# Padding the activation tiles by 64 bytes and shifting the low weight tiles by 32 in a float32r transformer kernel

## The chip, the cores and the metric

The kernel runs on one core of one Trainium2 chip. Its metric is the time of one launch on the device in microseconds (us). Before the change two timed runs took 3197.18 and 3197.62 us, a median of 3197.4 us.

## What is computed

Two layers of a first block (a state-space mixer beside multi-head latent attention, cross attention to a memory, a gated feed-forward network), then one layer of a second block (a compressed and windowed attention beside a dilated one, merged by gates), on 256 tokens of 2048 features in float32. Nearly all the work is products of 256 tokens with large weight matrices:

```python
proj = h @ w_in[l]                                   # 2048 x 3664
x = x + jnp.concatenate([y_ssd, y_mla], -1) @ w_out[l]
x = x + memory_cross_attention(h, m, w_xq[l], ...)
x = x + swiglu(h, w_gate[l], w_up[l], w_down[l])     # 2048 x 5632, twice, and back
...
proj = h @ w_in                                      # second block, 2048 x 11056
out = (sigmoid(ma) * ya + sigmoid(mb) * yb) @ w_out
```

## The kernel before

Each float32 operand of a long product is split into a high part of type float32r and a low part, the rest, also float32r. A product is then three matmuls into the same PSUM bank: high by high, high by low and low by high.

**Weights.** A block of a weight matrix comes by a transfer of SyncE's queue into a tile `raw` (pool `rawp`, 5 buffers). ScalarE copies it to `wh` (line 411) and VectorE subtracts that from `raw` to make `wl` (line 412). `wh` and `wl` come from one pool `wp`, 4 buffers for each name. A tile has 1024 elements, 4096 bytes, on each of 128 partitions.

**Activations.** A pair of tiles `xh`, `xl` holds 512 features of all 256 tokens, features on the partitions: 4 chunks of 256 tokens, 4096 bytes (pool `xp`, 6 buffers for each name, made by `pair`).

**The products.** `block` makes the products with the tokens on the output's partitions: the moving operand is a half of the weight tile, `wh[:, j]` or `wl[:, j]` with j = 0 or 1 (512 columns, 2048 bytes; where the block is 296 or 280 columns wide, the second half starts 1184 or 1120 bytes after the first), and the stationary operand is 128 tokens of a chunk of `xh` or `xl`, 512 bytes. It runs lines 423, 424 and 425 for the two token halves m of each j, so that six matmuls on j = 0 are followed by six on j = 1 (the last block of a product takes all of m = 0 first). `block_fm` is the other way round, for the state-space mixer's convolution inputs: 128 columns of weights are stationary and the 256 tokens of a chunk move (lines 461 to 463).

**Other work.** Norms, attention and the scan are cut into steps, "tasks", which `tick` places between the matmuls of the long products. The order on TensorE is the order in which the program is written; the other engines' order is made by a scheduler from priorities, and split work has a high one. Small temporaries come from pools `t2` (9 buffers of 2048 bytes) and `t1` (6 buffers, NT1). `t1` serves, among others, the convolution (line 791: a tile `u` of 3 + 256 columns whose first three GpSimd clears at line 792; lines 793 to 801 use it) and the block summaries of the second block (line 1321: copies of slices of `kc`, which TensorE then transposes at line 377).

**Where the tiles lie.** Pools take their memory one after the other, with the same address on every partition. By the built program, in bytes, with the distance between buffers:

| tile | before | after |
|---|---|---|
| `x`, the residual | 25,376 | 25,376 |
| `after_r`, a constant of the scan (line 887) | 44,384 | 44,384 |
| `raw` | 45,536 + 4096 i | 45,536 + 4096 i |
| `wh` | 66,016 + 4096 i | 66,016 + 4096 i |
| `wl` | 82,400 + 4096 i | 82,432 + 4096 i |
| `xh` | 98,784 + 4096 i | 98,816 + 4160 i |
| `xl` | 123,360 + 4096 i | 123,776 + 4160 i |
| slots (`ff`, `kc` and others) | 147,936 + 4096 i | 148,736 + 4096 i |
| `t2` | 197,088 + 2048 i | 197,888 + 2048 i |
| `t1` | 215,520 + 1056 i, i to 5 | 216,320 + 1056 i, i to 4 |

Modulo 512 bytes, `raw`, `wh`, `wl`, `xh`, `xl`, the slots and `t2` are all at 480 before the change. `x` is at 288, which is 192 below that, and `after_r` is at 352, which is 128 below.

Of the kernel before, what the change touches and what calls it, by code (L numbers as in the profile page):

```python
# [11 lines left out]
F32 = mybir.dt.float32  # L12
F32R = mybir.dt.float32r
# [6 lines left out]
P = 128  # L20
S = 256
# [6 lines left out]
NSLOT, NT2, NT1 = 12, 9, 6  # L28
# [6 lines left out]
# ---------------------------------------------------------------- host layout  # L35
# [6 lines left out]
def _tile_a(w, width=512):  # L42
    """[L, K, N] -> [L, N/width, K/512, 2, 128, 2, width]; one [128, 2, width] block per transfer."""
    L, K, N = w.shape
    w = w.reshape(L, K // 512, 2, 2, P, N // width, width)
    return np.ascontiguousarray(w.transpose(0, 5, 1, 2, 4, 3, 6))


def _tile_b(w):
    """[L, 2048, N] -> [L, N/128, 2, 128, 8, 128]."""  # L50
    L, K, N = w.shape
    w = w.reshape(L, 2, 8, P, N // P, P)
    return np.ascontiguousarray(w.transpose(0, 4, 1, 3, 2, 5))


def _cols(v):
    """[n*128] -> [128, n]"""
    return v.reshape(-1, P).T


def _rows(v):
    """[n] -> [128, n], the same row on every partition"""
    return np.broadcast_to(v.reshape(1, -1), (P, v.size))


def _feature_major(x):
    """[256, 2048] -> [128, 16, 256]"""
    return np.ascontiguousarray(x.T.reshape(16, P, S).transpose(1, 0, 2))


def _token_major(x):
    """[256, n] -> [128, 2, n]"""
    return np.ascontiguousarray(x.reshape(2, P, -1).transpose(1, 0, 2))
# [19 lines left out]
def _head_order_a():  # L93
    """Position p of a query head of branch a: pairs (g, g + 1) of key groups with one r."""
    return [(2 * (c // 4) + i) * 4 + c % 4 for c in range(8) for i in range(2)]
# [64 lines left out]
def _layout(a):  # L160
    """Every array that goes to the chip, in the order and the shape it is read."""
# [6 lines left out]
    w = a["w_in"]  # L168
# [5 lines left out]
    L = DEPTH  # L174
# [48 lines left out]
# ---------------------------------------------------------------- the program  # L223


class _Task:
    """Work beside the long products, cut into steps; a step yields the number of ticks to wait."""
# [5 lines left out]
class _Net:  # L233
    def __init__(self, ctx, tc, I, out, poff, coff):
        self.tc = tc
        self.nc = nc = tc.nc
        self.I = I
        self.out = out
        self.poff, self.coff = poff, coff
        self.now = 0  # L240
        self.ready = []
        self.tasks = []
        pool = lambda name, bufs, **k: ctx.enter_context(tc.tile_pool(name=name, bufs=bufs, **k))
        self.one = pool("one", 1)
        self.rawp = pool("rawp", 5)
        self.wp = pool("wp", 4)
        self.xp = pool("xp", 6)
        self.sp = pool("sp", NSLOT)
        self.k2 = pool("k2", NT2)
        self.k1 = pool("k1", NT1)  # L250
        self.sm = pool("sm", 1)
        self.psw = pool("psw", 4, space=PSUM)
        self.psm = pool("psm", 4, space=PSUM)
        ctx.enter_context(tc.manual_schedule(engines={mybir.EngineType.PE}))
        self.par = self.one.tile([P, I["params"].shape[1]], F32, name="par")
        self.cst = self.one.tile([P, I["consts"].shape[1]], F32, name="cst")
        self.x = self.one.tile([P, 2, D], F32, name="x")
        self.junk = self.one.tile([P, 512], mybir.dt.bfloat16, name="junk")
        self.mhalf = self.one.tile([P, 1], F32, name="mhalf")
        nc.gpsimd.memset(self.mhalf, -0.5)  # L260
        self.ident = self.c("ident")

    # -- tasks
# [17 lines left out]
    def get(self, t):  # L281
        """the result of a task, a list of them, or the value itself"""
        if isinstance(t, _Task):
            while not t.done:
                self.tick()
            return t.result
        return t
# [6 lines left out]
    # -- small things  # L294
# [30 lines left out]
    def rsqrt(self, out, ss, width):  # L325
        """out = (ss / width + eps) ** -0.5"""
        nc = self.nc
        n = ss.shape[1:]
        t = self.small([P] + list(n), name="rs" + "_".join(map(str, n)), bufs=2)
        nc.vector.tensor_scalar(t, ss, 1.0 / width, EPS, op0=OP.mult, op1=OP.add)  # L330
        mh = self.mhalf
        for _ in range(len(n) - 1):
            mh = mh.unsqueeze(1)
        nc.gpsimd.tensor_tensor(out, t, mh.to_broadcast([P] + list(n)), op=OP.pow)  # L334

    def squares(self, src, acc):
        """acc = sum of src ** 2 along the free axis"""
        self.nc.scalar.activation(self.junk[:, :src.shape[1]], src, AF.Square, accum_out=acc)

    def head_squares(self, src, acc, heads):  # L340
        """acc [128, heads] = sum of squares of every head's columns of src [128, 512]"""
        j = self.t2([P, 512])
        self.nc.scalar.activation(j, src, AF.Square)
        self.nc.vector.tensor_reduce(acc, j.rearrange("p (h d) -> p h d", h=heads), axis=AX.X, op=OP.add)

    # -- operands of the long products

    def pair(self):
        h = self.xp.tile([P, 4, S], F32R, name="xh", tag="xh")
        l = self.xp.tile([P, 4, S], F32R, name="xl", tag="xl")  # L350
        return h, l

    def hi_lo(self, pair, c, n, src, gain=None, imm=None):
        """chunks c .. c+n of a pair from src [128, n, 256], times a gain by partition"""
# [17 lines left out]
    def two_transposed(self, srcs):  # L372
        """srcs: two functions of the token tile giving [128 tokens, 128]; a bank [128, 2, 256]"""
# [9 lines left out]
    def transposed(self, src, gain=None, imm=None):  # L383
        """src(m) -> [128 tokens, 512]; a task for its four chunks, feature-major, as a pair"""
# [8 lines left out]
    def weights(self, src, n, w):  # L393
        """one block [128, n, w] from DRAM, split into high and low parts"""
# [6 lines left out]
    def weight_tiles(self, n, w):  # L401
        raw = self.rawp.tile([P, n, w], F32, name="raw", tag="raw")
        h = self.wp.tile([P, n, w], F32R, name="wh", tag="wh")
        l = self.wp.tile([P, n, w], F32R, name="wl", tag="wl")
# [9 lines left out]
    def block(self, pairs, srcs, w=512, hold=HOLD):  # L414
        """token-major products: two banks [128 tokens, w]; the last weights serve one bank, then the other"""
# [35 lines left out]
    def block_fm(self, pairs, src):  # L451
        """feature-major products for 128 columns: one bank [128 features, 256 tokens]"""
# [15 lines left out]
    # -- the residual stream  # L468
# [24 lines left out]
    # -- start  # L493

    def start(self):
        """the first operands, in the order they are needed"""
# [44 lines left out]
    def angles(self):  # L541
        """cosines and sines of every rotary embedding"""
# [45 lines left out]
    def rope_gains(self, l, which):  # L588
        """rotary tables with the gain of the rotated part folded in"""
# [12 lines left out]
    def rotate(self, out, x, ct, st):  # L602
        """out, x [128, ..., 2 * half] (up to three free axes), tables broadcast to the same shape"""
# [12 lines left out]
    # -- attention of one head  # L616

    def soft(self, s, mask, scale_of, spans):
        """spans [(lo, hi)] by query tile over the columns of a bank; returns exp and 1/sum"""
# [29 lines left out]
    def probs_t(self, e):  # L649
        """probabilities [128, 384] transposed: keys by [tile 0: all tokens | tile 1: second half]"""  # L650
# [9 lines left out]
    def scores(self, s, parts):  # L660
        """s [128, 384]; parts [(qT [k, 256], kT [k, 256])] sum over the contraction"""
# [6 lines left out]
    # ------------------------------------------------------------ block 1  # L668
# [72 lines left out]
    def rms_bank(self, r):  # L741
        """a column by token tile, as rows on every partition"""
# [13 lines left out]
    def ssd_steps(self, l, krd):  # L756
        """softplus of the step sizes, and the decays by step"""
# [48 lines left out]
    def ssd_scan(self, l, cb, dt, a):  # L806
# [24 lines left out]
        # masked c . b, state positions on the partitions  # L831
# [9 lines left out]
        # state after the first chunk  # L841
# [19 lines left out]
        def decays(m, g):  # L861
            """rows of summed decays for 8 heads"""
# [84 lines left out]
    def mla_queries(self, l, qa_t, rqa):  # L947
        """[nope heads 0-3, nope heads 4-7, rope of all heads] before the norm; -scale/rms by (tile, head)"""
# [68 lines left out]
    def mla_heads(self, l, hp, q, nsc, kn, kr, v):  # L1017
        """two heads: chunks of the pair that four heads share"""
# [38 lines left out]
    # -- attention to the memory  # L1057
# [34 lines left out]
    def head_rms(self, t, name):  # L1092
        """t [128, 2, 512]: 1/rms by (tile, head of 128)"""
# [84 lines left out]
    # -- feed forward  # L1178
# [45 lines left out]
    # ------------------------------------------------------------ block 2  # L1224
# [29 lines left out]
    def x_fm(self, nb):  # L1254
        """512 features of x times their gain, feature-major"""
# [9 lines left out]
    def h2_pair(self, nb, xt, rb):  # L1265
        """512 features of rms(x) * g_pre * (1 + scale) + shift"""
# [19 lines left out]
    def rope_part(self, t, c0, heads, dh, rot, tabs):  # L1286
        """rotate the first rot of every head's dh columns of t[:, :, c0:...] in place"""
# [3 lines left out]
    def gate_fm(self, pairs, src):  # L1291
        """twice silu of 4 feature-major chunks"""
# [10 lines left out]
    def plain_t(self, src, out):  # L1303
        """out [128, 4, 256] = four chunks of src(m), feature-major"""
# [5 lines left out]
    def summaries(self, t, c0, which, vc):  # L1310
        """block summaries of the columns c0.. (4 groups of 64) of t: [128 (group, 32), 64]"""
# [70 lines left out]
    def branch_a_inputs(self, pairs):  # L1382
# [11 lines left out]
        # a quarter of 1 + tanh: the gate, halved against the doubled silu  # L1394
# [7 lines left out]
    def branch_a_cmp(self, tasks, qt, ga, kcr):  # L1402
        """probabilities over the block summaries, gated: [128 (group, 32), r, tokens]"""
# [54 lines left out]
    def branch_a_heads(self, c, kts, qt, ks, kt, ga, cmp, vcr, zf):  # L1458
        """the two query heads of chunk c"""
# [43 lines left out]
    def branch_b(self, pairs, nb):  # L1503
        """inputs of 4 heads"""
# [35 lines left out]
    def gate_rows(self):  # L1540
        """gate * g_post along the free axis"""
# [136 lines left out]
```

## Time and profile before

| | |
|---|---|
| timed runs | 3197.18 and 3197.62 us |
| profiled execution, span | 3196.7 us |
| TensorE matmuls (PE) busy | 3175.3 us, 99% |
| TensorE weight loads (PEld) busy | 2656.9 us, 83% |
| VectorE (DVE) busy | 2034.1 us, 64% |
| ScalarE (ACT) busy | 1553.8 us, 49% |
| GpSimd (POOL) busy | 53.4 us, 2% |
| transfers | 625.28 MB, 196 GB/s |

Busy times of an engine are shares of the span in which at least one of its instructions runs. A matmul's recorded duration reaches past the start of the next, since matmuls are pipelined; times of one line therefore add up to more than the span. In a timeline the first column is the start of a row in us from the span's start and the second its duration.

### The profile page before, as it was taken

The numbers are of one execution on the slowest core, as the hardware profiler recorded it, in microseconds if no ns is written. First come the engines' busy times: TensorE is split into PE (matmuls) and PEld (weight loads), VectorE is DVE, ScalarE is ACT, GpSimd is POOL, SyncE is SP. The second block draws the span as 40 slices with busy tenths as digits, with TensorE's granted clock in tenths as the row PEclk, the third lists the DMA queues.
The fourth block names the chain that finished last, engine by engine and source line by source line (L and its number), as shares of the span: only waits on it lengthen the run. The fifth ranks groups of instructions, "written<-read, shape, count | busy, mean of one in ns | idle before, by whom it ended". The sixth has DMA issues, their size and how long they took to land.

```text
span 3196.7 us, 41513 instructions
## 1 busy us (share of the span) xinstructions
PE 3175.3 (99%) x15705; PEld 2656.9 (83%) x15705; DVE 2034.1 (64%) x3015; ACT 1553.8 (49%) x2191; POOL 53.4 (2%) x77
## 2 busy tenths in 40 slices
PE   9999999999999999999999999999999999999998
PEld 8987888888888889887888888888878977888887
DVE  6886665555555566885767677766765555455554
ACT  7465564444444455474654444444454455444443
POOL 0010000000000000010000000000000000000000
PEclk9999999999999999999999999999999999999999
DMA  8554555555555556454567777777746533555454
GB/s 299 172 169 145 186 172 187 192 192 191 192 187 192 191 175 189 159 183 141 190 228 265 266 270 270 253 250 269 269 143 219 174 105 99 179 184 180 162 184 151
DMA packets 175160, 625.28 MB, mean 196 GB/s; under 512 B 19696, under 2 KB 19952, under 8 KB 174704
## 3 DMA queue, kind: packets, MB, share of 16 engines
q1 hardware_dynamic: 173952, 620.26, 58.2%
q8 instruction: 123, 2.02, 0.3%
q10 hardware_dynamic: 1008, 2.37, 0.2%
q14 instruction: 77, 0.63, 0.1%
HBM read 620.46 MB, written 2.10 MB: 195 GB/s over the span
## 4 chain that ended last, share of the span: by engine, by line
PE 96%; DVE 1%; DMA 1%; issue 1%; POOL 0%; ACT 0%; SPq 0%; DVEq 0%; POOLq 0%; ACTq 0%
PE pw L423 27%; PE pw L425 27%; PE pw L424 27%; PE pw L461 2%; PE pw L462 2%; PE pw L463 2%; PE mb L377 2%; PE mb L665 2%; DMA wada<-w_ada 1%; PE mb L1493 1%; PE mb L1346 0%; PE mb L903 0%; DVE wl L412 0%; PE mb L1496 0%; PE mb L887 0%
## 5 line engine op out<-in xcount | busy, mean ns | idle before, releaser
L412 DVE TENSOR_TENSOR wl<-raw,wh 128x1024 fp32r<-128x1024 f32 (+3 forms) x1069 | 1285.6, 1204 | 969.7 <-ACT wh L411 967.2
L411 ACT ACTIVATE wh<-raw 128x1024 fp32r<-128x1024 f32 (+3 forms) x1069 | 1114.9, 1043 | 1384.8 <-PE pw L425 1258.0
L423 PE MATMUL pw<-wh,xh 128*128 128x512 f32 (+2 forms) x3952 | 1555.4, 394 | 6.2 <-ACT wh L411 4.9
L425 PE MATMUL pw<-wh,xl 128*128 128x512 f32 (+2 forms) x3952 | 1526.3, 386 | 0.0
L424 PE MATMUL pw<-wl,xh 128*128 128x512 f32 (+2 forms) x3952 | 1524.6, 386 | 0.6 <-DVE wl L412 0.6
L423 PEld LDWEIGHTS pw<-wh,xh 128*128 128x128 f32 x3952 | 744.2, 188 | 153.3 <-ACT wh L411 4.9
L425 PEld LDWEIGHTS pw<-wh,xl 128*128 128x128 f32 x3952 | 743.1, 188 | 150.7 <-DVE xl L368 0.7
L424 PEld LDWEIGHTS pw<-wl,xh 128*128 128x128 f32 x3952 | 744.6, 188 | 141.6 <-DVE wl L412 2.1
L461 PE MATMUL pw<-xh,wh 128*128 128x256 f32 x640 | 183.2, 286 | 0.0
L463 PE MATMUL pw<-xh,wl 128*128 128x256 f32 x640 | 181.2, 283 | 0.0
L462 PE MATMUL pw<-xl,wh 128*128 128x256 f32 x640 | 181.1, 283 | 0.0
L485 DVE TENSOR_TENSOR x<-x,pw 128x512 f32<-128x512 f32 x224 | 144.9, 679 | 3.8 <-PE pw L425 3.8
L1240 DVE CUSTOM_DVE_ANT_0 wada<-wada,crow 128x1024 f32<-128x1024 f32 x96 | 117.3, 1221 | 33.9 <-DMA wada<-w_ada 33.8
L461 PEld LDWEIGHTS pw<-xh,wh 128*128 128x128 f32 x640 | 122.7, 192 | 1.3 <-issue 0.8
L462 PEld LDWEIGHTS pw<-xl,wh 128*128 128x128 f32 x640 | 122.8, 192 | 0.1
L463 PEld LDWEIGHTS pw<-xh,wl 128*128 128x128 f32 x640 | 122.7, 192 | 0.0
L630 ACT ACTIVATE t<-t,mn 128x256 f32<-128x256 f32 (+1 forms) x128 | 58.4, 457 | 63.1 <-DVE mn L627 62.3
L367 ACT ACTIVATE xh<-mb,par 128x256 fp32r<-128x256 f32 x112 | 50.9, 467 | 13.1 <-PE mb L377 12.2
L368 DVE SCALAR_TENSOR_TENSOR xl<-mb,par,xh 128x256 fp32r<-128x256 f32 x112 | 51.8, 478 | 3.7 <-ACT xh L367 2.6
L334 POOL TENSOR_TENSOR xr<-rs,mhalf 128x1 f32<-128x1 f32 x16 | 9.8, 619 | 2512.1 <-DVE rs L330 2306.4
L358 ACT ACTIVATE xh<-mb 128x512 fp32r<-128x512 f32 (+1 forms) x68 | 35.1, 516 | 30.5 <-PE mb L377 15.8
L627 DVE CUSTOM_DVE_ANT_0 t<-mb,cst 128x128 f32<-128x128 f32 x80 | 26.0, 354 | 25.8 <-PE mb L665 25.4
(358 smaller groups left out, 1564.4 us busy)
## 6 DMA issues: line engine op xcount, KB each, us to landing
raw<-w_gate SPq DMA_DIRECT2D x176, 512.0 KB, 3.6
raw<-w_up SPq DMA_DIRECT2D x176, 512.0 KB, 3.8
raw<-w_down SPq DMA_DIRECT2D x176, 512.0 KB, 3.6
raw<-w_out SPq DMA_DIRECT2D x96, 512.0 KB, 3.5
wada<-w_ada SPq DMA_DIRECT2D x96, 512.0 KB, 5.5
raw<-w_in_x SPq DMA_DIRECT2D x48, 512.0 KB, 3.9
raw<-w_in_z SPq DMA_DIRECT2D x32, 512.0 KB, 3.5
raw<-w_ma SPq DMA_DIRECT2D x32, 512.0 KB, 3.3
```

Source lines behind the costliest of these rows:

```text
L377: self.nc.tensor.transpose(t[:, j, m * P:(m + 1) * P], src(m), self.ident)
L411: nc.scalar.activation(h, raw, AF.Copy)
L412: nc.vector.tensor_tensor(l, raw, h.bitcast(F32), op=OP.subtract)
L423: nc.tensor.matmul(pt[m], lhsT=xh[:, k, ms], rhs=wh[:, j], start=c == 0, stop=False)
L424: nc.tensor.matmul(pt[m], lhsT=xh[:, k, ms], rhs=wl[:, j], start=False, stop=False)
L425: nc.tensor.matmul(pt[m], lhsT=xl[:, k, ms], rhs=wh[:, j], start=False, stop=c == 4 * n - 1)
L461: nc.tensor.matmul(pt, lhsT=h[:, j], rhs=xh[:, c], start=(k == 0), stop=False)
L462: nc.tensor.matmul(pt, lhsT=h[:, j], rhs=xl[:, c], start=False, stop=False)
L463: nc.tensor.matmul(pt, lhsT=l[:, j], rhs=xh[:, c], start=False, stop=(k == 15))
L485: self.nc.vector.tensor_tensor(xs, xs, pt[m], op=OP.add)
L665: nc.tensor.matmul(s[:, a:b], lhsT=q[:, m * P:(m + 1) * P], rhs=k[:, 0:b - a], start=(i == 0), stop=(i == len(parts) - 1))
L1240: nc.vector.tensor_tensor_reduce(out=t, in0=t, in1=self.crow[hf], scale=1.0, scalar=0.0, op0=OP.mult, op1=OP.add, accum_out=self.adap[:, j ...
```

## The change

The `wl` tiles get a pool of their own behind a gap of 32 bytes. Each `xh` and `xl` tile gets 16 more elements, 64 bytes, at its end, which nothing reads or writes. With that, the stationary operands lie at 16 different offsets, multiples of 32 bytes modulo 512, from the moving ones, where they were at one before. To make room, the pool `t1` gets 5 buffers for 6. The rest of the diff takes comments out, and lines move by up to 3.

```diff
-NSLOT, NT2, NT1 = 12, 9, 6
+NSLOT, NT2, NT1 = 12, 9, 5
...
         self.wp = pool("wp", 4)
+        self.gap = pool("gap", 1)
+        self.gap.tile([P, 8], F32, name="gap")
+        self.wl_pool = pool("wl", 4)
         self.xp = pool("xp", 6)
...
     def pair(self):
-        h = self.xp.tile([P, 4, S], F32R, name="xh", tag="xh")
-        l = self.xp.tile([P, 4, S], F32R, name="xl", tag="xl")
-        return h, l
+        return tuple(self.xp.tile([P, 4 * S + 16], F32R, name=n, tag=n)[:, :4 * S].rearrange("p (c t) -> p c t", c=4)
+                     for n in ("xh", "xl"))
...
         h = self.wp.tile([P, n, w], F32R, name="wh", tag="wh")
-        l = self.wp.tile([P, n, w], F32R, name="wl", tag="wl")
+        l = self.wl_pool.tile([P, n, w], F32R, name="wl", tag="wl")
```

The order on TensorE, ScalarE, GpSimd and SyncE's queue is the same as before. On VectorE it differs only in the block summaries of the second block. Before, in the first of the two summaries (a number behind a tile's name is that of its buffer's use):

```order
L1321 COPY t_20406<-kc 128x128
L1321 COPY t_20408<-kc 128x128
L412 TENSOR_TENSOR wl<-raw,wh 128x560 x4
L412 TENSOR_TENSOR wl<-raw,wh 128x1024 x4
L1395 TENSOR_SCALAR ga<-ga 128x96
L412 TENSOR_TENSOR wl<-raw,wh 128x1024
L1336 TENSOR_TENSOR blk<-mb,par 64x8x15 x8
L1321 COPY t_20410<-kc 128x128
L412 TENSOR_TENSOR wl<-raw,wh 128x1024
L1321 COPY t_20412<-kc 128x128
```

Now, at the same place (numbers of tiles are 7 higher, lines 2):

```order
L1323 COPY t_20413<-kc 128x128
L414 TENSOR_TENSOR wl<-raw,wh 128x560 x4
L414 TENSOR_TENSOR wl<-raw,wh 128x1024 x4
L1397 TENSOR_SCALAR ga<-ga 128x96
L414 TENSOR_TENSOR wl<-raw,wh 128x1024
L1338 TENSOR_TENSOR blk<-mb,par 64x8x15 x8
L1323 COPY t_20415<-kc 128x128
L414 TENSOR_TENSOR wl<-raw,wh 128x1024
L1323 COPY t_20417<-kc 128x128
L1323 COPY t_20419<-kc 128x128
```

One copy, of the second half of the third group, has moved from before nine splits of weight blocks to behind them, so that two copies stand together behind the next split where one did. In the second summary, some 50 us later, two copies move behind one split each.

## Rows read from the trace of the kernel before

**Rows 1.** The page, parts 1 and 2: busy us, and granted clock in 40 slices.

```profile
PE 3175.3 (99%) x15705; PEld 2656.9 (83%) x15705; DVE 2034.1 (64%) x3015; ACT 1553.8 (49%) x2191; POOL 53.4 (2%) x77
PEclk9999999999999999999999999999999999999999
```

**Rows 2.** Waits of PE: who waited for whom, us in total, times, longest.

```profile
PE pw L423 <- ACT wh L411: 4.9, 1, 4.9
...
PE pw L423 <- DVE x L485: 0.3, 1, 0.3
```

**Rows 3.** Groups of PE by shape: line, tiles, shape, count, busy us, mean ns.

```profile
L423 PE MATMUL pw<-wh,xh 128*128 128x512 f32 x3760 | 1497.9, 398 | 6.2 <-ACT wh L411 4.9 <-ACT xh L1275 1.1 <-DVE x L485 0.3
...
L461 PE MATMUL pw<-xh,wh 128*128 128x256 f32 x640 | 183.2, 286 | 0.0
...
L423 PE MATMUL pw<-wh,xh 128*128 128x296 f32 x128 | 38.7, 302 | 0.0
...
L423 PE MATMUL pw<-wh,xh 128*128 128x280 f32 x64 | 18.8, 295 | 0.0
```

**Rows 4.** Timeline of PE in the feed-forward network: start us, duration, line.

```profile
1026.74 0.39 PE L423 MATMUL pw<-wh,xh 128*128 128x512 f32 x1
...
1027.19 0.39 PE L425 MATMUL pw<-wh,xl 128*128 128x512 f32 x1
...
1030.82 0.39 PE L423 MATMUL pw<-wh,xh 128*128 128x512 f32 x1
```

**Rows 5.** Timeline of PE in the convolution's products.

```profile
99.73 0.28 PE L463 MATMUL pw<-xh,wl 128*128 128x256 f32 x1
...
101.89 0.28 PE L463 MATMUL pw<-xh,wl 128*128 128x256 f32 x1
```

**Rows 6.** Timeline of PEld, the weight loads, at the place of rows 4.

```profile
1027.19 0.19 PEld L423 LDWEIGHTS pw<-wh,xh 128*128 128x128 f32 x1
```

**Rows 7.** Timeline of PE in blocks of 296 columns, first of each six.

```profile
33.31 0.30 PE L423 MATMUL pw<-wh,xh 128*128 128x296 f32 x1
...
34.13 0.30 PE L423 MATMUL pw<-wh,xh 128*128 128x296 f32 x1
...
34.95 0.30 PE L423 MATMUL pw<-wh,xh 128*128 128x296 f32 x1
```

**Rows 8.** Timeline of PE in blocks of 280 columns, first of each six.

```profile
2394.90 0.29 PE L423 MATMUL pw<-wh,xh 128*128 128x280 f32 x1
...
2395.67 0.29 PE L423 MATMUL pw<-wh,xh 128*128 128x280 f32 x1
...
2396.44 0.29 PE L423 MATMUL pw<-wh,xh 128*128 128x280 f32 x1
```

**Rows 9.** Timeline of PE where transpositions of x and ff follow a product.

```profile
341.29 0.39 PE L425 MATMUL pw<-wh,xl 128*128 128x512 f32 x1
341.52 0.60 PE L377 MATMUL mb<-cst,x 128*128 128x128 f32 x4
...
501.25 0.39 PE L425 MATMUL pw<-wh,xl 128*128 128x512 f32 x1
501.48 0.60 PE L377 MATMUL mb<-cst,ff 128*128 128x128 f32 x4
```

**Rows 10.** Timeline of PE at the scan's decays.

```profile
152.52 1.10 PE L887 MATMUL mb<-ar,after 128*128 128x512 f32 x4
153.45 0.39 PE L423 MATMUL pw<-wh,xh 128*128 128x512 f32 x1
```

**Rows 11.** Timelines of DVE and PE at two users of t1.

```profile
1248.91 0.48 DVE L798 SCALAR_TENSOR_TENSOR t<-t,cw,t 128x256 f32<-128x256 f32 x1
1250.28 0.42 DVE L793 TENSOR_TENSOR t<-pw,t 128x256 f32<-128x256 f32 x1
...
2429.69 0.22 DVE L1321 COPY t<-kc 128x128 f32<-128x128 f32 x1
...
2431.32 0.60 PE L377 MATMUL mb<-cst,t 128*128 128x128 f32 x4
```

## The prediction

> **What bounds the kernel now.** The busy times come first: TensorE is busy for 3175.3 of 3196.7 us, and its granted clock stays in the top tenth of full speed in all 40 slices [rows 1], which is the 2.4 GHz level. Then the waits of TensorE: eleven kinds, the longest one 4.9 us in total and the shortest 0.3 us, 12.4 us together [rows 2]. So nothing that TensorE waits for is worth more than 0.4%, and the time is the number of matmuls times the distance from the start of one to the start of the next. I call that distance the step. The durations in the grouped rows are longer (398 ns for 512 columns [rows 3]) because neighbouring matmuls overlap; the step has to be read from a timeline.
>
> The grouped rows give the counts: each shape has three lines of equal count (423 to 425, or 461 to 463), so there are 3 x 3760 = 11,280 matmuls of 512 columns, 3 x 640 = 1,920 of 256, 3 x 128 = 384 of 296 and 3 x 64 = 192 of 280 [rows 3]. That is 13,776 in all. Steps: at 512 columns, the first and last row of 19 stand 4.08 us apart, 18 steps of 226.7 ns [rows 4]. At 256 columns, 19 rows stand 2.16 us apart, 18 steps of 120.0 ns [rows 5]. The sum: 11,280 x 226.7 = 2557 us, 1,920 x 120.0 = 230 us, 384 x 136.7 = 52 us and 192 x 128.3 = 25 us (the last two steps are read below), 2864 us or 90% of the span. The rest is the small attention matmuls, the transpositions and the start.
>
> The two long steps also show what is in a step. They differ by 106.7 ns for 256 columns, 0.417 ns a column, one column per cycle at 2.4 GHz. What is left at no columns is 120.0 - 106.7 = 13.3 ns. This fixed part, 13,776 x 13.3 = 183 us or 5.7% of the time, is the only thing that where the operands lie could touch. While a matmul streams its moving operand (wh or wl), the weights of the next (xh or xl) are loaded: the load recorded at 1027.19 starts as the matmul before its own does [rows 4, 6], so both read the same memory at once, and a bank collision would show up as such a fixed part.
>
> **Part one: the operands get 16 offsets.** Before, wh, wl, xh and xl all start at the same place modulo 512 bytes, and chunks, token halves and the half j of a 512-wide block are multiples of 512 apart: offset 0 in every pair. If the 13.3 ns came from that, a pair at another offset would step faster. The trace of before already holds such pairs.
>
> First, blocks of 296 columns. Half j = 1 starts 296 x 4 = 1184 bytes after j = 0, which is 160 modulo 512. Six matmuls of j = 1 run from 33.31 to 34.13 us, six of j = 0 from 34.13 to 34.95: 0.82 us each, 136.7 ns a step [rows 7]. Without the fixed part a step would be 296 x 0.417 = 123.4 ns, six of them 0.74 us. The j = 1 half does not lose it.
>
> Second, blocks of 280 columns, where j = 1 lies at 1120 bytes, 96 modulo 512. Six of j = 0 take 2394.90 to 2395.67, six of j = 1 take 2395.67 to 2396.44: 0.77 us each, 128.3 ns [rows 8], against 6 x 116.8 = 0.70 us without the fixed part.
>
> Third, a 512-column matmul during which the weights of a transposition are loaded. With weights from x, at offset 192, the step is 341.29 to 341.52; with weights from ff, at offset 0, it is 501.25 to 501.48: 0.23 us both times [rows 9].
>
> Fourth, the 512-column matmuls of line 887, with both operands in other pools and 128 between them: four take 152.52 to 153.45, 232.5 ns each [rows 10]. That is a little more than 226.7, like the 0.23 us beside a transposition at offset 0, and no trace of 213.
>
> So 0, 96, 128, 160 and 192 behave alike, both multiples of 64 and odd multiples of 32. There is a reason to expect it of the others: while 512 bytes of weights are loaded, recorded with 0.19 us [rows 6], the moving operand runs through most of its 2048 bytes in a step of 0.227 us. The distance between the two addresses grows by more than 512 bytes during one load, so whatever offset they start from, they pass through all 16. I take a gain of nothing for the change of offsets. Bounds from the same rows: a row is printed to 0.01 us, and a run of six is known to 1.7 ns a step; 13,776 x 1.7 = 23 us either way.
>
> The trace shows 226.7 ns at 512 columns. The Trainium skill, in "TensorE: Matmul & The Clock Gate", section "Back-to-back issue gap", gives a warm step of N / 2.4 + 2.5 ns, which is 215.8 at 512 and 109.2 at 256. The trace disagrees by 10.9 and 10.8 ns; by that rule nearly all of the fixed part ought to be removable, and the sum, if this change removed it, would be an estimate of 3197 - (11,280 x 10.9 + 1,920 x 10.8 + 384 x 10.9 + 192 x 9.1) / 1000 = 3048 us. Nothing in the trace ties that difference to the offset.
>
> **Part two: what else the shift touches.** The padded rows hold the same 1024 elements, and no instruction is added. The subtraction that writes wl now writes 32 bytes off from what it reads; no row shows a price for that. Its cover: VectorE is busy for 2034.1 of 3196.7 us [rows 1], so its work may take half as long again before it fills the span. I take nothing. The tiles behind xp move by 800 bytes, and the raw tiles, which take the weight transfers, not at all.
>
> **Part three: five t1 buffers instead of six.** Where does a sixth buffer matter? I set each t1 tile's first write against the last read of the tile whose buffer it now gets. Two places come out late. In the convolution the clearing of three columns on GpSimd (line 792) must now wait for the third multiply-add of the channel before, line 798, which starts at 1248.91 and takes 0.48 us. What needs the cleared tile is line 793, at 1250.28 [rows 11]: done with 0.8 us to spare, and GpSimd has nothing else queued there. In the block summaries, one more copy of 0.22 us is held on VectorE until the first transpositions have read their tiles, so that two copies stand together where the last one stood alone. It ran from 2429.69 to 2429.91; the last of two now ends about 2430.13, and the transpositions that need it start at 2431.32 [rows 11]. Queued behind it are splits of weight blocks that TensorE wants later. Cost nothing; if the cover were gone, the copy's 0.2 us, and with all of its kind below 3 us.
>
> The sum: 0 + 0 + 0 on a profiled span of 3196.7 us, whose two timed runs have a median of 3197.4. So 3197.4 us.
>
> **The rivals.** *Faster: the fixed part is a collision after all.* It would have to be one that the offsets 96, 128, 160 and 192 share with 0 and the other 11 of the 16 do not. Against it stand rows 7 to 10; for it only that the fixed part has no other visible cause and that the trace shows no pair of split operands at, say, 64 or 256. If 11 of 16 lost it: 183 x 11 / 16 = 126 us, 3071 us. If all did: 3014 us. This turns into over 2% from 64 us / 13,776 = 4.6 ns a step. (The Trainium skill's step, in the section named above, would put this case at the estimate of 3048 us.)
>
> *Slower: equal offsets are the good case.* Two streams in lock step might avoid each other, and an unequal offset cost a few ns. The nearest row for that is line 887, 232.5 against 226.7 at offset 128 [rows 4, 10]: 5.8 ns x 13,776 = 80 us, 3277 us. Against it: the steps of rows 9 are as long at offset 0, and rows 7 and 8 show no rise at 160 and 96. It decides from 4.6 ns a step, too.
>
> *A wait in place of the buffer.* If the five buffers hold up ScalarE's or VectorE's queue, TensorE sees it only after the blocks that are split ahead are used up. Against it: part three. Time: at most 3200 us, no change.
>
> **How the numbers follow.** No change, 0.9: four independent places say so, and TensorE waits for nothing that the change could lengthen. The collision rival 0.06, the lock-step rival 0.04. About 2% is what a measurement of this kernel can tell from no change, and the cases fall on its sides as named. The range is the forecast's own, 3197.4 less and plus the 23 us of the steps' resolution: 3174 to 3220; it leaves the two rivals outside, 0.10, and some of the 0.9.
>
> **What would show it.** In the profile after, the steps of 512 and 256 columns in an undisturbed stretch: 226.7 and 120.0 if I am right, 213 to 222 if the collision rival is, 230 and more for the other. If the offsets matter singly, steps would differ within one block between lines 423, 424 and 425, or from one x tile to the next. TensorE's waits should stay near 12 us, with no new one on the summaries' transpositions. I am wrong if the fixed part depends on an offset that no row here holds.

## The result, and the profile after

The changed kernel takes 3235.9 us (two runs, 3235.59 and 3236.21), against 3197.4 before: a ratio of 1.012, with a 95% interval of 1.0077 to 1.0164. It is slower by 38.5 us, which is less than 2% but more than the measurement's uncertainty, and 16 us above the end of the predicted range. The profiled execution has a span of 3233.3 us, 36.6 more than the 3196.7 of before.

The page of the kernel after, span and busy times (they answer to [rows 1]):

```profile
span 3233.3 us, 41527 instructions
...
PE 3212.4 (99%) x15705; PEld 2652.1 (82%) x15705; DVE 2036.2 (63%) x3015; ACT 1553.7 (48%) x2191; POOL 53.1 (2%) x77
```

TensorE has the same 15,705 matmuls and is busy 37.1 us longer; VectorE, ScalarE and GpSimd are within 2.1 us of before. The mean granted clock is 0.998 of full speed, the 2.4 GHz level. The waits of TensorE after, the longest and the shortest of ten kinds (as [rows 2]; a row gives us in total, times, longest):

```profile
PE pw L425 <- ACT wh L413: 5.2, 2, 4.5
...
PE mb L379 <- DVE mg L1610: 0.3, 1, 0.3
```

The ten add up to 12.1 us, where there were 12.4, and none is on the block summaries' transpositions. So TensorE does not wait longer; its steps are longer. The groups of PE by shape (as [rows 3], whose lines 423 and 461 are 425 and 463 here):

```profile
L425 PE MATMUL pw<-wh,xh 128*128 128x512 f32 x3760 | 1516.8, 403 | 6.2 <-ACT wh L413 5.2 <-ACT xh L1277 1.1
L426 PE MATMUL pw<-wl,xh 128*128 128x512 f32 x3760 | 1476.7, 393 | 0.8 <-DVE wl L414 0.8
L427 PE MATMUL pw<-wh,xl 128*128 128x512 f32 x3760 | 1476.6, 393 | 0.0
L463 PE MATMUL pw<-xh,wh 128*128 128x256 f32 x640 | 181.8, 284 | 0.0
```

The line that was 1497.9 us, 398 ns, is now 1516.8 us, 403 ns; the line of 256 columns went the other way, 183.2 to 181.8. The timeline of PE in the feed-forward network after (start us, duration, line; as [rows 4]), four rows that follow one another and the one 81 steps behind the first:

```profile
1026.10 0.40 PE L425 MATMUL pw<-wh,xh 128*128 128x512 f32 x1
1026.34 0.39 PE L426 MATMUL pw<-wl,xh 128*128 128x512 f32 x1
1026.57 0.39 PE L427 MATMUL pw<-wh,xl 128*128 128x512 f32 x1
1026.79 0.40 PE L425 MATMUL pw<-wh,xh 128*128 128x512 f32 x1
...
1044.82 0.40 PE L425 MATMUL pw<-wh,xh 128*128 128x512 f32 x1
```

81 steps take 18.72 us, 231.1 ns each, where there were 226.7. Within a triple the steps are about 0.24, 0.23 and 0.22 us: they differ by line. The convolution's products after (as [rows 5]), 42 steps apart:

```profile
99.01 0.28 PE L463 MATMUL pw<-xh,wh 128*128 128x256 f32 x1
...
103.95 0.28 PE L463 MATMUL pw<-xh,wh 128*128 128x256 f32 x1
```

That is 4.94 / 42 = 117.6 ns, where there were 120.0. At 256 columns the change is a gain.

To see where the 36.6 us are, I took every distance from one matmul's start to the next in both traces, instruction by instruction in the same order, and summed the differences by line. A step belongs to the matmul that streams while the weights of the next are loaded, so the pair of operands that meet in it is the streamed tile of one row and the loaded tile of the next:

| step of | streams, loads meanwhile | count | mean change | sum |
|---|---|---|---|---|
| L425, 512 columns | `wh`, `xh` | 3760 | +5.5 ns | +20.6 us |
| L426, 512 columns | `wl`, `xl` | 3760 | +2.7 ns | +10.2 us |
| L427, 512 columns | `wh`, `xh` of the next chunk or half | 3760 | +2.6 ns | +9.6 us |
| L463 to L465, 256 columns | x tiles, weights | 1920 | -1.6 ns | -3.0 us |
| all others | | | | -0.3 us |

The sum is +37.0 us; the spans differ by 36.6, so nothing of size is left elsewhere. Blocks of 296 and 280 columns, which a cost common to all widths would have lengthened too, moved by less than 0.2 us together.

### The profile page after: what moved, and what is told of

Its sections match the earlier page's. It is cut to its first block, busy times and chain, and to the rows that moved or that the text cites. A ratio compares the mean times of both kernels' runs of the same rounds, so it can differ in the third digit from the quotient of the medians.

```text
span 3233.3 us, 41527 instructions
## 1 busy us (share of the span) xinstructions
PE 3212.4 (99%) x15705; PEld 2652.1 (82%) x15705; DVE 2036.2 (63%) x3015; ACT 1553.7 (48%) x2191; POOL 53.1 (2%) x77
## 4 chain that ended last, share of the span: by engine, by line
PE 97%; DVE 1%; issue 1%; POOL 0%; ACT 0%; DMA 0%; SPq 0%; DVEq 0%; POOLq 0%; ACTq 0%
PE pw L425 28%; PE pw L426 27%; PE pw L427 27%; PE pw L463 2%; PE pw L465 2%; PE pw L464 2%; PE mb L379 2%; PE mb L667 2%; PE mb L1495 0%; PE mb L1348 0%; PE mb L905 0%; PE mb L1498 0%; PE mb L889 0%; PE mb L655 0%; DVE wl L414 0%
## 5 line engine op out<-in xcount | busy, mean ns | idle before, releaser
L425 PE MATMUL pw<-wh,xh 128*128 128x512 f32 (+2 forms) x3952 | 1574.3, 398 | 6.2 <-ACT wh L413 5.2
L426 PE MATMUL pw<-wl,xh 128*128 128x512 f32 (+2 forms) x3952 | 1533.5, 388 | 0.8 <-DVE wl L414 0.8
L427 PE MATMUL pw<-wh,xl 128*128 128x512 f32 (+2 forms) x3952 | 1533.5, 388 | 0.0
L427 PEld LDWEIGHTS pw<-wh,xl 128*128 128x128 f32 x3952 | 742.6, 188 | 171.2 <-DVE xl L370 0.7
L425 PEld LDWEIGHTS pw<-wh,xh 128*128 128x128 f32 x3952 | 743.5, 188 | 164.1 <-ACT wh L413 5.6
L426 PEld LDWEIGHTS pw<-wl,xh 128*128 128x128 f32 x3952 | 743.7, 188 | 151.2 <-DVE wl L414 1.8
L463 PE MATMUL pw<-xh,wh 128*128 128x256 f32 x640 | 181.8, 284 | 0.0
L465 PE MATMUL pw<-xh,wl 128*128 128x256 f32 x640 | 179.9, 281 | 0.0
L463 PEld LDWEIGHTS pw<-xh,wh 128*128 128x128 f32 x640 | 120.5, 188 | 1.3 <-issue 0.8
L465 PEld LDWEIGHTS pw<-xh,wl 128*128 128x128 f32 x640 | 120.4, 188 | 0.0
```

Of the source, the lines that this page charges most:

```text
L425: nc.tensor.matmul(pt[m], lhsT=xh[:, k, ms], rhs=wh[:, j], start=c == 0, stop=False)
L426: nc.tensor.matmul(pt[m], lhsT=xh[:, k, ms], rhs=wl[:, j], start=False, stop=False)
L427: nc.tensor.matmul(pt[m], lhsT=xl[:, k, ms], rhs=wh[:, j], start=False, stop=c == 4 * n - 1)
L463: nc.tensor.matmul(pt, lhsT=h[:, j], rhs=xh[:, c], start=(k == 0), stop=False)
L465: nc.tensor.matmul(pt, lhsT=l[:, j], rhs=xh[:, c], start=False, stop=(k == 15))
```

## The experiments

Four theories were to be told apart. **Buffer**: the fifth `t1` buffer costs it. **Pair**: a step is set by the distance, in bytes, from the place where the streamed operand starts to the place of the weights loaded meanwhile. **Sequence**: a change of place from one matmul to the next costs, so that a constant distance costs nothing. **Place**: what counts is where the tiles lie, or the padding, not their distance. A later one, **Pair by width**, has the good distance depend on the number of columns. "Distance" is loaded minus streamed from here on; the offsets of the prediction carry no sign, and rows 7 to 10, by this rule, hold distances of -160, -96, -192 and -128 bytes. All but the two of cells were timed beside the kernel before, on the same chip.

**The buffer alone (nt1_five).**

```diff
-NSLOT, NT2, NT1 = 12, 9, 6
+NSLOT, NT2, NT1 = 12, 9, 5
```

> Only the t1 pool of the change: five buffers, every weight and activation tile where it was. If the loss comes from the fifth buffer (theory Buffer): about 3236 us. If it comes from where the operands lie (all other theories): 3197 us, within 3 us, and steps of 226.7 ns at 512 columns.

3197.36 us, a ratio of 1.0001 (0.9991 to 1.0010). Buffer falls. All changed forms of the kernel below but two (pad_256 and fm_64, which take the room from `rawp`) have this edit as well; the two of cells are kernels of their own.

**The padding alone (pad_only).** The low weights are not shifted, so distances are multiples of 64.

```diff
-        h = self.xp.tile([P, 4, S], F32R, name="xh", tag="xh")
-        l = self.xp.tile([P, 4, S], F32R, name="xl", tag="xl")
-        return h, l
+        return tuple(self.xp.tile([P, 4 * S + 16], F32R, name=n, tag=n)[:, :4 * S].rearrange("p (c t) -> p c t", c=4)
+                     for n in ("xh", "xl"))
```

> Five t1 buffers and the 64-byte pad, the low weights not shifted: wh and wl start at one place modulo 512, the x tiles at eight multiples of 64 from it. Theory Pair (every offset between streamed operand and loaded weights costs, constant or not): all three lines dearer, 3230 to 3245 us. Theory Sequence (only operands that lie differently from one matmul to the next cost): the place changes at each xh to xl and at each new x tile, not between wh and wl: part of the loss, 3205 to 3230 us. Theory Place (starts at an even multiple of 32 instead of an odd one cost): no start is moved off its odd multiple of 32, so 3197 us.

3242.11 us, 1.0139 (1.0122 to 1.0156). The steps of 512 columns rose by 3.0, 4.4 and 5.4 ns for the three lines, 48.1 us; those of 256 columns fell by 2.1, 4.0 us. Half of the change costs as much as the whole: the two intervals overlap.

**The shift alone (wl_32).** `wl` lies 32 bytes off; a second gap of 480 bytes puts the x tiles back on their old offset.

```diff
+        self.gap = pool("gap", 1)
+        self.gap.tile([P, 8], F32, name="gap")
+        self.wl_pool = pool("wl", 4)
+        self.gap2 = pool("gap2", 1)
+        self.gap2.tile([P, 120], F32, name="gap2")
...
-        l = self.wp.tile([P, n, w], F32R, name="wl", tag="wl")
+        l = self.wl_pool.tile([P, n, w], F32R, name="wl", tag="wl")
```

> Five t1 buffers, the low weights 32 bytes further, a second gap of 480 behind them, so that all x tiles stay where they were modulo 512: offset 32 for the middle line alone. Theory Pair: only the line that streams wl is dearer, by some 4 ns, 3760 x 4 ns = 15 us, so 3212 us. Theory Sequence: both changes, wh to wl and wl to wh, cost: 3215 to 3230 us, and the line that streams wh at an offset of 0 is dearer too. Theory Place: wl starts at an even multiple of 32, a third of the loss, 3210 us, on the wl line alone.

3238.62 us, 1.0127 (1.0112 to 1.0142). Its timeline at the place of [rows 4], lines 428 to 430 being the triple, 24 steps from the first row to the last:

```profile
1026.11 0.39 PE L428 MATMUL pw<-wh,xh 128*128 128x512 f32 x1
1026.34 0.40 PE L429 MATMUL pw<-wl,xh 128*128 128x512 f32 x1
1026.58 0.39 PE L430 MATMUL pw<-wh,xl 128*128 128x512 f32 x1
1026.80 0.39 PE L428 MATMUL pw<-wh,xh 128*128 128x512 f32 x1
...
1031.65 0.39 PE L428 MATMUL pw<-wh,xh 128*128 128x512 f32 x1
```

Only the middle line has a pair whose distance changed. Over the whole trace its step, steps into other work left out, is 235.9 ns (+8.6, 32.5 us). But the line ahead of it, whose own pair is as before, also rose, by 3.4 ns to 231.1 (12.7 us); the third stayed at 227.1. Pair alone gave 3212 us, all of it on the middle line. The rise of a neighbour is what Sequence foresaw, but 3238.62 us is above its 3215 to 3230 as well, so neither gives the size.

**One constant distance (x_32 and x_160).** All x tiles move by 32 or by 160 bytes, weights stay: every split pair has the same new distance, and nothing is padded. The edit of x_32 is shown; in x_160 one gap of `[P, 40]` stands there and `wl` stays in `wp`.

```diff
+        self.wl_pool = pool("wl", 4)
+        self.gap2 = pool("gap2", 1)
+        self.gap2.tile([P, 8], F32, name="gap2")
...
-        l = self.wp.tile([P, n, w], F32R, name="wl", tag="wl")
+        l = self.wl_pool.tile([P, n, w], F32R, name="wl", tag="wl")
```

> Five t1 buffers and a gap of 32 bytes ahead of the x tiles: every x tile at offset 32 from wh and wl, the same for all matmuls. Theory Pair: all lines dearer alike, 3220 to 3245 us. Theory Sequence: nothing changes from one matmul to the next, so 3197 us. Theory Place: the stationary operands all start at even multiples of 32, up to the full loss, 3236 us.

> Five t1 buffers and a gap of 160 bytes ahead of the x tiles: 160 between streamed operand and loaded weights in every long product, the distance that cost nothing in the blocks of 296 columns. The prediction's reading, carried to 512 columns: 3197 us. Theory Pair by width: 512-column steps of 229 to 236 ns, so 3220 to 3290 us, and 256-column steps below 120.

x_32: 3253.93 us, 1.0176 (1.0161 to 1.0191). Its timeline, six steps of 512 columns, then 33 of 256:

```profile
1025.78 0.40 PE L428 MATMUL pw<-wh,xl 128*128 128x512 f32 x1
...
1027.18 0.40 PE L428 MATMUL pw<-wh,xl 128*128 128x512 f32 x1
```

```profile
98.99 0.28 PE L464 MATMUL pw<-xh,wh 128*128 128x256 f32 x1
...
102.83 0.28 PE L464 MATMUL pw<-xh,wh 128*128 128x256 f32 x1
```

1.40 / 6 = 233.3 ns and 3.84 / 33 = 116.4 ns. All three lines of 512 columns are alike now, 61.7 us more in sum, and the 256-column steps give 5.7 us back. x_160 gave 3259.27 us, 1.0192 (1.0177 to 1.0207): 512 columns again at 232.8 to 233.8 ns (+64.2 us), 256 columns at 118.5, and its blocks of 296 columns as before (their halves hold 160 and 0 here, 0 and -160 before). One single distance, the same for all, costs more than the change's mixture (12 distances meet at 512 columns). Sequence gave 3197 us for a constant distance, so it falls in the form in which it was put; Pair had 3220 to 3245 us for x_32, which is too low by 9.

**Everything moved alike (all_32).** The gap stands ahead of `wp`, so all the split tiles move by 32 bytes and distances stay.

```diff
+        self.gap = pool("gap", 1)
+        self.gap.tile([P, 8], F32, name="gap")
         self.wp = pool("wp", 4)
```

> Five t1 buffers and a gap of 32 bytes ahead of the wh tiles: wh, wl, xh and xl all start at even multiples of 32, at distance 0 from each other. Theory Pair: 3197 us and 226.7 ns. Theory Place (the start itself counts): 3220 us or more.

3197.76 us, 0.9999 (0.9989 to 1.0009). Place falls; padding is tested by itself below (pad_256).

**The step by itself (steps).** A small kernel that only runs cells of 24 matmuls in a row, one distance and one width to a cell.

```python
for i in range(24):
    k = b + 128 * (i % 4)
    nc.tensor.matmul(t[:, 0:n], lhsT=s[:, k:k + 128], rhs=w[:, a:a + n], start=i == 0, stop=i == 23)
```

> A kernel that computes nothing of the reference: after 96 matmuls to warm up, cells of 24 float32r matmuls each, every one with its own weight load, the streamed operand w and the loaded weights s at a set distance modulo 512 bytes. Eighteen distances from 0 to 496 at 512, 256, 296, 280 and 384 columns, then both operands moved alike, then only the streamed one. Theory Pair by width (the cost hangs on the distance and on the number of columns together): at 512 columns 226.7 ns at distance 0 and 228 to 236 at the others; at 256 columns 120 at 0 and 116 to 119 at the others; at 296 and 280 columns 136 and 128 to 130 at all distances. Theory Sequence (a constant distance costs nothing): the same step at every distance of a width. Both moved alike: the step of distance 0 by Pair, a dearer one if it is the place itself that counts.

Its timeline of PE; a row is a cell, and a step is the distance to the next row's start over 24. First 512 columns, distances 0, 16, 32, 64, then 160, 192, 224, 256, 288 (the row behind each ends it):

```profile
33.38 5.60 PE L55 MATMUL pb<-w,s 128*128 128x512 f32 x24
38.82 5.61 PE L55 MATMUL pa<-w,s 128*128 128x512 f32 x24
44.27 5.75 PE L55 MATMUL pb<-w,s 128*128 128x512 f32 x24
49.86 5.76 PE L55 MATMUL pa<-w,s 128*128 128x512 f32 x24
...
66.67 5.77 PE L55 MATMUL pb<-w,s 128*128 128x512 f32 x24
72.27 5.67 PE L55 MATMUL pa<-w,s 128*128 128x512 f32 x24
77.78 5.76 PE L55 MATMUL pb<-w,s 128*128 128x512 f32 x24
83.37 5.61 PE L55 MATMUL pa<-w,s 128*128 128x512 f32 x24
88.82 5.75 PE L55 MATMUL pb<-w,s 128*128 128x512 f32 x24
```

5.44 us at distance 0 is 226.7 ns; 5.59 at 32 is 232.9; 5.60 at 160 is 233.3; 5.51 at 192 is 229.6; 5.45 at 256 is 227.1, and from there it repeats. The cells of 64, 96 and 128 take 233.3 to 233.8. With both operands moved alike by 32, 64 or 256 bytes the step is 227 to 228. With the streamed one moved by 64 (distance -64, which is 192 modulo 256) it is 229.6, as at 192. So at 512 columns what counts in these cells is the distance modulo 256, and no distance is better than 0. A constant distance costs by itself, against Sequence once more. Then 256 columns at distances 0 and 64; 296 columns at 0 and 352, which is the -160 of [rows 7]; and 280 columns at 0 and 416, the -96 of [rows 8]:

```profile
133.36 3.03 PE L55 MATMUL pb<-w,s 128*128 128x256 f32 x24
136.24 3.01 PE L55 MATMUL pa<-w,s 128*128 128x256 f32 x24
...
141.92 2.89 PE L55 MATMUL pa<-w,s 128*128 128x256 f32 x24
144.64 3.05 PE L55 MATMUL pb<-w,s 128*128 128x256 f32 x24
...
184.44 3.43 PE L55 MATMUL pb<-w,s 128*128 128x296 f32 x24
187.71 3.44 PE L55 MATMUL pa<-w,s 128*128 128x296 f32 x24
...
223.63 3.42 PE L55 MATMUL pb<-w,s 128*128 128x296 f32 x24
226.89 3.44 PE L55 MATMUL pa<-w,s 128*128 128x296 f32 x24
...
243.22 3.23 PE L55 MATMUL pb<-w,s 128*128 128x280 f32 x24
246.28 3.28 PE L55 MATMUL pa<-w,s 128*128 128x280 f32 x24
...
286.48 3.25 PE L55 MATMUL pb<-w,s 128*128 128x280 f32 x24
289.57 3.21 PE L55 MATMUL pa<-w,s 128*128 128x280 f32 x24
```

At 256 columns distance 0 is dear, 2.88 / 24 = 120.0 ns, and 64 is cheap, 2.72 / 24 = 113.3. At 296 columns 0 and 352 are alike, 136.3 and 135.8 ns (160 takes 137.1), though the width has its own spread (133.3 at 32 and 192, 139.2 at 64), which the expectation did not have. At 280 columns 0 and 416 take 127.5 and 128.8 (96 takes 129.6). The width decides which distance is good.

**Finer, and in the kernel's order (steps_fine).** Cells at 8-byte and 16-byte distances, and cells that repeat the kernel's triple with one tile moved.

```python
k = b[i % 3] + 128 * (i // 3 % 4)
nc.tensor.matmul(t, lhsT=s[:, k:k + 128], rhs=w[:, a[i % 3]:a[i % 3] + 512], start=i == 0, stop=i == 23)
```

> Computes nothing of the reference, like the first kernel of cells. Distances from 0 to 256 in steps of 8 and a few of 4 at 512 columns; 0 to 496 in steps of 16 and four around 64 at 256 columns; the other half of the streamed tile; and five cells of triples in the kernel's order (high by high, low by high, high by low). Theory Pair by width: at 512 columns 226.7 ns near 0 and near 256, 228.9 at 192, 233 elsewhere, and nothing below 226.7; at 256 columns 113.3 at 64 and nothing below. If only the streaming and the loaded operand count, each by itself, the triple with the low weights 32 further is one dear step in three, (226.7 x 2 + 233.4) / 3 = 228.9 ns; if a change of place between neighbours costs as well, about 231.5, which is a third of 694.5, the sum of the three lines' steps that the kernel with the low weights shifted showed. The triple with the low activations 256 further: 226.7; 384 further: 229 or more.

No distance gave 512 columns a step under 226.7 ns. But the expectation's 226.7 near 0 and near 256 does not hold: 8 bytes already take 5.54 / 24 = 230.8 ns and 248 bytes 233, while 120 bytes are as good as 0, 5.45 / 24 = 227.1. The rows of 8 and 120, each with the one behind it:

```profile
39.19 5.71 PE L54 MATMUL pa<-w,s 128*128 128x512 f32 x24
44.73 5.76 PE L54 MATMUL pb<-w,s 128*128 128x512 f32 x24
...
117.43 5.61 PE L54 MATMUL pa<-w,s 128*128 128x512 f32 x24
122.88 5.75 PE L54 MATMUL pb<-w,s 128*128 128x512 f32 x24
```

The triples, in its timeline: all at 0, low weights by 32, low x by 384, low x by 256, all loaded tiles by 32:

```profile
358.36 5.61 PE L59 MATMUL pb<-w,s 128*128 128x512 f32 x24
363.81 5.72 PE L59 MATMUL pa<-w,s 128*128 128x512 f32 x24
369.38 5.71 PE L59 MATMUL pb<-w,s 128*128 128x512 f32 x24
374.92 5.61 PE L59 MATMUL pa<-w,s 128*128 128x512 f32 x24
380.37 5.76 PE L59 MATMUL pb<-w,s 128*128 128x512 f32 x24
```

The first four take 5.45, 5.57, 5.54 and 5.45 us to the next start, 227.1, 232.1, 230.8 and 227.1 ns a step; the fifth has no row behind it, and its own 23 steps average 233.1. One moved pair in three at 233.3 and two at 226.7 would make 228.9; the 232.1 says that the neighbours of a moved pair pay too, as in wl_32. Not all cells agree between the two kernels: distance 16 at 512 columns is 38.82 to 44.27 in the first (227.1 ns), and in the second it runs from the row at 44.73 above to this one:

```profile
50.33 5.68 PE L54 MATMUL pa<-w,s 128*128 128x512 f32 x24
```

That is 233.3 ns. The 256-column cells at 96 (120.4 and 117.1) and 320 also differ, as do some others: 320, which is 64 modulo 256, took 117.9 ns in the first and 113.8 in the second. The cell before was another one, so what a cell begins with seems to matter; that was not tested by itself.

**Padding that keeps the good distances (pad_256).** If the distance modulo 256 decides, padding by 256 bytes costs nothing.

```diff
-        self.rawp = pool("rawp", 5)
+        self.rawp = pool("rawp", 4)
...
+        return tuple(self.xp.tile([P, 4 * S + 64], F32R, name=n, tag=n)[:, :4 * S].rearrange("p (c t) -> p c t", c=4)
+                     for n in ("xh", "xl"))
```

> The x tiles padded by 256 bytes instead of 64, the low weights not shifted, six t1 buffers, and four raw buffers instead of five to make room: the distances are 0 and 256. Theory Pair by width, with the period of 256 that the cells show at 512 columns: 3197 us and 226.7 ns. If it is the padding, or that tiles lie unevenly, whatever the distance: 3220 us or more. If four raw buffers are too few: new waits of TensorE for ScalarE's copies.

3197.98 us, 1.0001 (0.9991 to 1.0010). 24 steps of its timeline:

```profile
1026.20 0.39 PE L422 MATMUL pw<-wh,xh 128*128 128x512 f32 x1
...
1031.64 0.39 PE L422 MATMUL pw<-wh,xh 128*128 128x512 f32 x1
```

5.44 / 24 = 226.7 ns. It is not the padding, and not that tiles lie at different offsets modulo 512.

**Each width at its own distance (fm_64).** Weight blocks that go to the convolution (128 columns wide, stationary there) lie 64 bytes further in; all else stays at 0.

```diff
-        self.rawp = pool("rawp", 5)
+        self.rawp = pool("rawp", 4)
...
+        o = 16 if w == P else 0
+        h, l = (self.wp.tile([P, 1024 + 128], F32R, name=t, tag=t)[:, o:o + n * w].rearrange("p (a b) -> p a b", a=n)
+                for t in ("wh", "wl"))
```

> Meant to beat both kernels. The weight tiles get 512 bytes more, and the products of 256 columns (and they alone) use them 64 bytes further in, so that the loaded weights start 64 beyond the streamed tokens; everything of 512 columns stays at distance 0; four raw buffers make the room. Theory Pair by width: 256-column steps of 113.3 instead of 120.0, 1,920 x 6.7 = 12.8 us less, 3184.6 us. If a constant distance is not what counts in the kernel: 3197 us.

3188.42 us, 0.9972 (0.9961 to 0.9984), faster than both kernels: by 0.28% than the one before, which is small but outside the interval. 33 steps in the convolution:

```profile
98.92 0.28 PE L462 MATMUL pw<-xh,wh 128*128 128x256 f32 x1
...
102.66 0.28 PE L462 MATMUL pw<-xh,wh 128*128 128x256 f32 x1
```

3.74 / 33 = 113.3 ns, as in the cell. Over all 1,920 steps the gain is 5.5 ns on average, 10.6 us, where 6.7 ns and 12.8 us were expected: some 300 of the 1,920 steps took 116 to 120 ns, and why was not followed further. The steps of 296 columns took 1.1 us more, all of it in three steps between 32.2 and 33.7 us, so it is a single delay at the start and no price of a distance.

## Why the prediction was wrong

**The bound** was read rightly: TensorE's steps are the time. Before and after, its waits are 12 us, and the 36.6 us of the spans are all in steps.

**Part one failed**, and the step of it that failed is "so 0, 96, 128, 160 and 192 behave alike". It put five offsets, seen at three widths and partly beside a transposition, into one statement and carried that to 512 columns.

- [Rows 7, 8] were read correctly as far as they resolve: at 296 columns a distance of -160 takes 135.8 ns in the cells against 136.3 at 0, at 280 columns -96 takes 128.8 against 127.5. But at 512 columns 160 costs 6.6 ns, and -160, which is 96 modulo 256, costs 7. Nothing in those rows says that widths may be exchanged, and [rows 4, 5] were the only rows for the two widths that fill the kernel, both at one distance.
- [Rows 9] could not decide: the distance to x is -192, which is 64 modulo 256 and costs 6.6 ns in a 512-column cell, but a row resolves 10, and x and ff both print 0.23. The trace of before as a whole would not have helped: its 46 undisturbed steps ahead of a transposition of x average 231.7 ns and its 44 ahead of one of ff, at distance 0, 231.9. Both load float32 weights, so they are no measure for a pair of float32r tiles.
- [Rows 10] pointed the right way: 512 columns, float32r, four steps that average 232.5 ns, three of them at distance -128 and the last, which loads an x tile, at 0. The cell of 128 takes 233.3. It was the only row of before with several steps of the kernel's main width at another distance, it stood 5.8 ns above 226.7, well beyond its resolution of 2.5 ns, and I called it "a little more" and set it beside the 0.23 of rows 9.
- The argument that the two operands "pass through all 16" during one load is refuted by the cells: distances of 0 and 32 at the start differ by 6 ns a step and more, although the streamed address runs on by 2048 bytes either way.

**The bounds** failed with it. The 23 us were the resolution of six-step rows for distances that do nothing, so the range had nothing in it for a distance that does. The fixed part was priced as something that could only be lost; at 512 columns it grew, from 13.4 ns to up to 20.

**The lock-step rival**, "equal offsets are the good case", was right at 512 columns in sign, in mechanism as far as the runs go, and, for a single distance, in size: its 5.8 ns a step stand against 61.7 us / 11,280 = 5.5 ns in x_32 and 64.2 / 11,280 = 5.7 ns in x_160. Its time of 3277 us is too high for two reasons. It priced all 13,776 matmuls, where 256 columns gain and 296 and 280 do nothing. And the mean rise at 512 columns is 40.4 us / 11,280 = 3.6 ns, under its own point of 4.6 ns a step for 2%. That a few pairs of the mixture land at 0 or 192 does not explain so small a rise: with the cells' prices its pairs would still cost 5.8 ns in the mean. Its chance of 0.04 was too low; rows 10 were the best evidence at the main width, and they spoke for it.

**The collision rival** was right at other widths: at 256 columns half of the 13.3 ns goes at distance 64, 13.3 to 6.6, and at 296 columns 3 ns go at 32 and 192. At 512 columns no distance tried removed any.

**Parts two and three** held. VectorE is busy 2036.2 us against 2034.1, though `wl` is written 32 bytes off, and the five buffers cost nothing (nt1_five).

**What the runs leave open.** The price per pair does not add up in a mixture. With the cells' prices for each of the after kernel's 11,280 pairs the sum is 66 us, where the trace has 40.4; for pad_only it is 44 against 48.1, for wl_32 24 against 43.8. In the trace after, steps at distance 0 average 231.2 ns and at 192 227.7, and those at 32 run from 226 to 235. Grouping by a step's own distance (modulo 256) leaves a scatter of 3.1 ns of 3.5, by its own and the one before 2.6. So neighbours carry part of it, and what they carry was not found. That a distance matters is shown; which time a given mixture of distances takes is not, and neither is why the same cell takes two different steps behind two different cells. Nor is it shown what the two operands contend for; the runs show only that moving one against the other changes the step and moving both alike does not.

## What to carry to other kernels

Where TensorE is the bound, read the step between matmul starts for each width by itself, and take evidence on a tile's place only from rows of the same width. Before moving or padding operand tiles, measure the step in a small cell at that width and distance; here tiles kept equal modulo 256 bytes were as good as any for 512 float32r columns, and 64 bytes apart best for 256. Keep the sign of an offset, since -192 and 192 are different distances. A lone row that stands above its resolution at the very width in question calls for a test, whatever several others at other widths say.

## What the runs showed of the hardware

With float32r operands at the 2.4 GHz level, a 512-column step is 226.7 ns at a distance of 0 or 256 bytes between the streamed operand and the weights loaded meanwhile, 229 to 230 at 192, and 233 at most others; a 256-column step is 120.0 at 0 and 113.3 at 64 (steps, and the kernels x_32 and fm_64). Less one column per cycle, that is 13.4 to 20 ns and 6.6 to 13.3 ns beside the columns. A shift of 32 bytes is worth 1.8% of this kernel's time (x_32).

The Trainium skill, in "SBUF — State Buffer", section "Who interferes with whom", gives TensorE two independent read ports, one for the moving operand and one for the weights, and says "PE and ACT never wait on anyone." No other engine was needed here for a step to change, so the runs don't speak on other engines; but if the independence of the two ports is to mean that a load never slows the stream beside it, steps of 226.7 and 233.3 ns that differ only in where the weights lie do not agree with it.
